# Prompt attention: diagonal blocks first in each unit, and the order 3, 2, 0, 1 for the last head and the output

## The chip, the cores and the metric

The kernel runs on one core of a Trainium2 chip. The metric is device time in microseconds (us) of one execution; lower is better. All tensors are float32. The engines are named as the profile names them: PE (TensorE, matmuls), DVE (VectorE), ACT (ScalarE), POOL (GpSimd) and SP (SyncE, which here only issues DMAs). Each engine works through its own instructions strictly in the order in which the program lists them; engines wait for one another through semaphores.

## The reference, cut to what matters

One layer of a hybrid decoder: a prompt of 2048 tokens and 64 sample tokens go through an input projection, a latent attention with 8 heads (MLA), a gated linear attention (GLA), an output projection, a gated addition and a norm. The change touches the attention of the prompt, and the order in which the output stage takes the prompt's tiles.

```python
def block(args):
    qn_b, qr_b, start = args
    s = (jnp.einsum('bqhd,bkhd->bhqk', qn_b, k_nope)
         + jnp.einsum('bqhr,bkr->bhqk', qr_b, k_rope)).astype(jnp.float32) * scale
    qpos = start + jnp.arange(Q_BLOCK)
    s = jnp.where(kpos[None, :] <= qpos[:, None], s, -jnp.inf)
    p = jax.nn.softmax(s, axis=-1).astype(v.dtype)
    return jnp.einsum('bhqk,bkhd->bqhd', p, v)
...
h = h + jnp.concatenate([o_mla, o_gla], axis=-1) @ w_out
h = h + jax.nn.sigmoid(h @ w_ple_gate) * (p_l @ w_ple_proj)
```

## The kernel before, in words

The kernel runs in stages: projections and GLA (to about 790 us of the span), then the attention of the prompt with the attention of the sample tokens (`decode`) woven into its first heads, then the output stage (`output`), tile by tile.

**Units.** The attention of the prompt is cut into 32 units (h, j): head h from 0 to 7, and for each head the query tile j of 512 queries, in the order `JS = (3, 2, 1, 0)`. A unit (h, j) reads the keys up to its own last query: 4j + 4 blocks of 128 keys. The 4j earlier blocks are full (512 queries wide). The last four lie on the diagonal: they are 512, 384, 256 and 128 queries wide, and a triangle of 128 x 128 in each has to be set to zero. So a unit with j = 0 has nothing but diagonal blocks.

**One block** (`attend`, L944): three matmuls make the scores in a PSUM tile `psC` of which there are two (L955 to L957); two exponentials on ACT write `ph`, rounded for the matmul, and `pf`, in full precision (L959, L961); a subtraction on DVE makes the low part `pl` from both (L963); in a diagonal block two selects on POOL zero the triangle, first of `ph`, then of `pl` (L966); then three matmuls, called PV here, add to the output tile `poC` (L968 to L970). There is **one** `poC` (`bufs=1`): the next unit's first PV waits until ACT has copied it out as `ob` (L973). A tile of `psC` is free again when `pf` has been made from it. The reading of `ph` by the subtraction comes before the select of `ph`, so a select waits for L963.

**The maxima** of the next unit (`maxima`, L915) run between the blocks of the current one: matmuls into `pmC` (L925), reductions on DVE (L927, L930, L932), and at the end a negation (L937), four small matmuls that turn the result (L940) and a copy by ACT into row 96 of the next unit's queries (L941), without which its first scores cannot start.

**After a unit** `ob` goes to DRAM: the values to `Od`, the sums to `Dd` (L974, L975). After the last unit of a head, and after every unit of head 7, the sums are read back (L980), inverted on DVE (L981) and written to `Rd` (L982).

**The output stage** splits its weights into a high part (on POOL, `gcopy`, L52) and a low part (DVE, L61). The first of them, from `in_w_out`, go into the places of keys and values that are already free, while head 7 still runs: they are loaded into `VT0`, head 6's values, once (6, 0) has finished. For each tile of 128 tokens `mix` (L1068) loads `Od`, `Gd`, `Rd` and `MGd` into four tiles `raw` (L1072 to L1079), multiplies on POOL (L1082) and DVE (L1083), and transposes on PE into `ptE` (L1087); `outproj` and `ple` are matmuls into `pgE`. The first three tiles' `mix` is begun while head 7 runs.

**The order of the work** on each engine is made when the program is built: a scheduler with a model of the time places the instructions, so the order around a place can change although the code there does not.

## Time and profile before

| | |
|---|---|
| median of 3 runs | 1880.7 us (1877.29 to 1881.57) |
| the profiled execution | 1881.52 us; its span, from the first instruction to the last, 1879.5 us |
| mean granted clock of PE in it | 0.955 |
| chain that ended last, PE's share | 70% |

The page counts a matmul as busy for the whole time from its start to its modelled end. Matmuls overlap, so the time at which the next one starts is what counts, and a wait of PE is longer than the idle time that the page shows for it. The page's PE row shows some digits below 9 within the span: at the start, around 750 to 800 us, and between 1375 and 1425 us, where attention ends and the output begins.

The view of stretches gives busy time of each engine and the granted clock in any part of the span. The timeline lists instructions one by one with the idle time before them and what ended it. Both are used below.

### The profile page before, as it was taken

What the parts mean: (1) busy time and instruction counts of PE and PEld (TensorE: products, weight loads), DVE (VectorE), ACT (ScalarE), POOL (GpSimd) and SP (SyncE); (2) the same over time, 40 slices, a digit from 0 to 9 for tenths busy, and PEclk for the clock granted to TensorE, in tenths of its full rate; (3) what the DMA queues carried; (4) which work ended last, traced back from release to release, by engine and by line L of the source; (5) the groups of instructions that cost most, each with busy time, mean ns of one, the idle gap of its engine ahead of it and who ended that gap; (6) DMA issues with size and microseconds to landing.
All of it is one profiled execution on the core that took longest, in us unless ns stands there. A gap on an engine that the chain in (4) does not pass through costs nothing.

```text
span 1879.5 us, 26843 instructions
## 1 busy us (share of the span) xinstructions
PE 1749.4 (93%) x8928; PEld 1365.5 (73%) x8928; DVE 1080.3 (57%) x2359; ACT 781.7 (42%) x1896; POOL 532.3 (28%) x915
## 2 busy tenths in 40 slices
PE   4999987899999998499999999999999999999996
PEld 3877776688887786266666777777777888888884
DVE  6376476466653666466666687777777333333323
ACT  4354365343431433055554666766661212121212
POOL 5253253333442334424343011111136000000000
PEclk7999989899999998699999999999998999999998
DMA  5164475511111114655666243123334223322111
GB/s 170 40 241 140 163 272 183 170 42 40 45 40 48 32 35 121 195 157 155 184 172 171 62 129 89 49 69 77 91 84 147 89 75 88 95 85 82 56 49 34
DMA packets 187748, 200.53 MB, mean 107 GB/s; under 512 B 23290, under 2 KB 130668, under 8 KB 187612
## 3 DMA queue, kind: packets, MB, share of 16 engines
q1 hardware_dynamic: 180956, 177.86, 32.3%
q0 software_dynamic: 6656, 20.98, 3.6%
q8 instruction: 71, 1.16, 0.3%
q14 instruction: 65, 0.53, 0.1%
HBM read 142.42 MB, written 56.35 MB: 106 GB/s over the span
## 4 chain that ended last, share of the span: by engine, by line
PE 70%; DMA 3%; DVE 3%; issue 2%; SPq 1%; POOL 1%; ACT 1%; POOLq 0%; ACTq 0%; DVEq 0%
PE pgE L64 7%; PE pgE L66 7%; PE pgE L65 7%; PE pgB L66 4%; PE pgB L64 4%; PE pgB L65 4%; PE psC L955 3%; PE poC L968 3%; PE pmC L925 3%; PE poC L970 3%; PE psC L957 3%; PE psC L956 3%; PE poC L969 3%; PE ptD L783 2%; PE poD L82 1%
## 5 line engine op out<-in xcount | busy, mean ns | idle before, releaser
L959 ACT ACTIVATE ph<-psC 128x512 fp32r<-128x512 f32 (+1 forms) x320 | 171.5, 536 | 206.1 <-PE psC L957 90.1
L963 DVE TENSOR_TENSOR pl<-pf,ph 128x512 fp32r<-128x512 f32 (+1 forms) x320 | 191.3, 608 | 58.5 <-ACT pf L961 49.2
L961 ACT ACTIVATE pf<-psC 128x512 f32<-128x512 f32 (+1 forms) x320 | 170.9, 534 | 0.0
L927 DVE TENSOR_REDUCE mxC<-pmC 128x1 f32<-128x512 f32 x192 | 128.9, 684 | 54.0 <-PE pmC L925 38.1
L955 PE MATMUL psC<-qC,KT 97*128 97x512 f32 (+1 forms) x320 | 124.1, 388 | 15.4 <-issue 11.8
L966 POOL TENSOR_SCALAR_AFFINE_SELECT ph<-ph 128x128 fp32r<-128x128 f32 x128 | 43.3, 339 | 322.5 <-DVE pl L963 228.0
L968 PE MATMUL poC<-ph,VT 128*128 128x512 f32 (+1 forms) x320 | 124.3, 388 | 8.8 <-POOL ph L966 6.7
L925 PE MATMUL pmC<-KT,qC 96*128 96x512 f32 (+2 forms) x320 | 119.2, 399 | 10.1 <-issue 4.6
L970 PE MATMUL poC<-pl,VT 128*128 128x512 f32 (+1 forms) x320 | 122.0, 382 | 1.3 <-DVE pl L963 1.3
L956 PE MATMUL psC<-qC,KT 96*128 96x512 f32 (+1 forms) x320 | 119.6, 374 | 0.0
L957 PE MATMUL psC<-qC,KT 96*128 96x512 f32 (+1 forms) x320 | 119.5, 373 | 0.0
L969 PE MATMUL poC<-ph,VT 128*64 128x512 f32 (+1 forms) x320 | 118.1, 369 | 0.0
L955 PEld LDWEIGHTS psC<-qC,KT 97*128 97x128 f32 x320 | 61.3, 192 | 38.4 <-issue 13.4
L1139 DVE SCALAR_TENSOR_TENSOR thE<-thE,pgE 128x512 f32<-128x512 f32 x32 | 22.0, 688 | 114.3 <-ACT thE L1138 114.3
L64 PE MATMUL pgE<-wpg,hh 128*128 128x512 f32 x224 | 87.7, 392 | 0.0
L65 PE MATMUL pgE<-wpg,hh 128*128 128x512 f32 x224 | 87.7, 392 | 0.0
L925 PEld LDWEIGHTS pmC<-KT,qC 96*128 96x128 f32 x320 | 62.6, 198 | 32.3 <-issue 11.0
L1138 ACT ACTIVATE thE<-pgE 128x512 f32<-128x512 f32 x32 | 19.1, 598 | 160.6 <-PE pgE L66 160.6
L66 PE MATMUL pgE<-wpg,hl 128*128 128x512 f32 x224 | 85.3, 392 | 0.0
L968 PEld LDWEIGHTS poC<-ph,VT 128*128 128x128 f32 x320 | 62.7, 196 | 29.0 <-POOL ph L966 13.4
L775 POOL DMA_INDIRECT kt<-in_kropeT,idk x64 | 61.5, 961 | 65.5 <-PE ptD L787 49.5
L61 DVE TENSOR_TENSOR x<-x 128x512 fp32r<-128x512 f32 (+2 forms) x74 | 64.6, 917 | 22.8 <-PE pgB L65 14.2
(456 smaller groups left out, 4674.7 us busy)
## 6 DMA issues: line engine op xcount, KB each, us to landing
x<-in_xT SPq DMA_DIRECT2D x32, 512.0 KB
ct<-in_ckvT SPq DMA_DIRECT2D x256, 64.0 KB
x<-in_w_in SPq DMA_DIRECT2D x16, 512.0 KB
Qn<-qq SPq DMA_DIRECT2D x16, 512.0 KB
Kn<-qq SPq DMA_DIRECT2D x16, 512.0 KB
Vd<-qq SPq DMA_DIRECT2D x16, 512.0 KB
KT<-Kn SPq DMA_DIRECT2D x32, 256.0 KB
VT<-Vd SPq DMA_DIRECT2D x8, 1024.0 KB
```

What stands on the lines that cost most here:

```text
L64: T_.matmul(out, ah, bh, start=first, stop=False)
L65: T_.matmul(out, ah, bl, start=False, stop=False)
L66: T_.matmul(out, al, bh, start=False, stop=last)
L925: T_.matmul(ps[:, :w], qs, kv[0][cb][:96, 0, :w], start=True, stop=True)
L955: T_.matmul(ps[:, c0:], kh[:, ks], qh[:, c0:], start=True, stop=False)
L956: T_.matmul(ps[:, c0:], kh[:96, ks], ql[:, c0:], start=False, stop=False)
L957: T_.matmul(ps[:, c0:], kl[:, ks], qh[:96, c0:], start=False, stop=True)
L959: A.activation(ph[:, c0:], ps[:, c0:], AF.Exp, scale=SC)
L963: V.tensor_tensor(pl[:, c0:], pf[:, c0:], ph[:, c0:].bitcast(F32), op=ALU.subtract)
L968: T_.matmul(o[:, c0:], vt[:, kb, DV:192], ph[:, c0:], start=kb == 0, stop=False)
L969: T_.matmul(o[:DV, c0:], vt[:, kb, 0:DV], ph[:, c0:], start=False, stop=False)
L970: T_.matmul(o[:, c0:], vt[:, kb, DV:192], pl[:, c0:], start=False, stop=kb == nk - 1)
```

## The change

In `attend` the loop over the key blocks now starts with the four diagonal blocks and then takes the full ones; the flags that open and close the accumulation follow the new first and last block. Head 7 takes its query tiles in the order 3, 2, 0, 1 (`LAST`), and the output stage takes its tiles in the same order, so that its last prompt tiles are those of j = 1. The arithmetic of each block, the number of matmuls, exponentials, selects and DMAs, and their sizes are the same.

```diff
-            for kb in range(nk):
+
+            for n, kb in enumerate(list(range(4 * j, nk)) + list(range(4 * j))):
                 dg = kb - 4 * j
...
-                T_.matmul(o[:, c0:], vt[:, kb, DV:192], ph[:, c0:], start=kb == 0, stop=False)
+                T_.matmul(o[:, c0:], vt[:, kb, DV:192], ph[:, c0:], start=n == 0, stop=False)
                 T_.matmul(o[:DV, c0:], vt[:, kb, 0:DV], ph[:, c0:], start=False, stop=False)
-                T_.matmul(o[:, c0:], vt[:, kb, DV:192], pl[:, c0:], start=False, stop=kb == nk - 1)
+                T_.matmul(o[:, c0:], vt[:, kb, DV:192], pl[:, c0:], start=False, stop=n == nk - 1)
...
-            if h == H - 1 or j == 0:
+            if h == H - 1 or j == JS[-1]:
                 n = 4 if h == H - 1 else 16
-                view = slice(j * 512, j * 512 + n * P)
+                c0 = j * 512 if h == H - 1 else 0
+                view = slice(c0, c0 + n * P)
...
-        units = [(h, j) for h in range(H) for j in JS]
+        units = [(h, j) for h in range(H) for j in (JS if h < H - 1 else LAST)]
...
-            tiles = [(j * 4 + q, P) for j in JS for q in range(4)] + [(NT, SD)]
+            tiles = [(j * 4 + q, P) for j in LAST for q in range(4)] + [(NT, SD)]
...
 JS = (3, 2, 1, 0)
+LAST = (3, 2, 0, 1)
```

The lines of `attend` after the loop's head stand one lower in the changed file, those of the output stage two lower (the scores are L956 to L958, the PV matmuls L969 to L971, the select L967, `ob` L974, `mix`'s product on POOL L1084). In the rows below a number behind a name tells one tile from another.

**Place 1, PE and ACT between two heads**, from (4, 0) to (5, 3). `poC_12191` is the output tile of (4, 0), `psC_12347` the first scores of (5, 3), `qC_12188` its queries, `m4r_12322` its maxima. PE before:

```order
L968 MATMUL poC_12191<-ph_12255,VT0_6777 128x256
L969 MATMUL poC_12191<-ph_12255,VT0_6777 64x256
L940 MATMUL pmC_12324<-identr_73,m4r_12322 1x128 x4
L925 MATMUL pmC_12375<-KT10_6773,qC_12343 128x512
L970 MATMUL poC_12191<-pl_12259,VT0_6777 128x256
L968 MATMUL poC_12191<-ph_12295,VT0_6777 128x128
L969 MATMUL poC_12191<-ph_12295,VT0_6777 64x128
L970 MATMUL poC_12191<-pl_12299,VT0_6777 128x128
L955 MATMUL psC_12347<-qC_12188,KT10_6773 128x512
```

PE after the change, and behind it ACT there, before and after:

```order
L969 MATMUL poC_12191<-ph_12295,VT0_6777 128x128
L970 MATMUL poC_12191<-ph_12295,VT0_6777 64x128
L971 MATMUL poC_12191<-pl_12299,VT0_6777 128x128
L940 MATMUL pmC_12324<-identr_73,m4r_12322 1x128 x4
L925 MATMUL pmC_12379<-KT10_6773,qC_12343 128x512
L956 MATMUL psC_12347<-qC_12188,KT13_6776 128x512
```

```order
L961 ACTIVATE pf_12257<-psC_12251 128x256
L959 ACTIVATE ph_12295<-psC_12291 128x128
L961 ACTIVATE pf_12297<-psC_12291 128x128
L941 ACTIVATE qC_12188<-pmC_12324 1x512
L973 ACTIVATE ob_12330<-poC_12191 128x512
L959 ACTIVATE ph_12351<-psC_12347 128x512
```

```order
L962 ACTIVATE pf_12257<-psC_12251 128x256
L960 ACTIVATE ph_12295<-psC_12291 128x128
L962 ACTIVATE pf_12297<-psC_12291 128x128
L974 ACTIVATE ob_12330<-poC_12191 128x512
L941 ACTIVATE qC_12188<-pmC_12324 1x512
L960 ACTIVATE ph_12351<-psC_12347 128x512
```

The small matmuls of the maxima moved behind the last PV of the unit, and on ACT the copy of the maxima moved behind `ob`.

**Place 2, POOL at the start of head 7.** `KT00` to `KT03` are the first places of the output's weights, `VT0` holds what was loaded for them; `ph_14376`, `ph_14391` and `ph_14430` belong to the first diagonal blocks of (7, 3) after the change, `ph_14614` to the first diagonal block of (7, 3) before it. Before:

```order
L52 TENSOR_SCALAR KT00_15230<-VT0_15211 128x512
L52 TENSOR_SCALAR KT01_15233<-VT0_15211 128x512
L52 TENSOR_SCALAR KT02_15237<-VT0_15211 128x512
L52 TENSOR_SCALAR KT03_15240<-VT0_15211 128x512
L966 AFFINE_SELECT ph_14614<-ph_14614 128x128
```

After the change:

```order
L52 TENSOR_SCALAR KT00_15230<-VT0_15211 128x512
L52 TENSOR_SCALAR KT01_15233<-VT0_15211 128x512
L52 TENSOR_SCALAR KT02_15237<-VT0_15211 128x512
L52 TENSOR_SCALAR KT03_15240<-VT0_15211 128x512
L967 AFFINE_SELECT ph_14376<-ph_14376 128x128
L967 AFFINE_SELECT pl_14380<-pl_14380 128x128
L52 TENSOR_SCALAR KT13_15244<-VT0_15211 128x512
L967 AFFINE_SELECT ph_14391<-ph_14391 128x128
```

The four splits stand where they stood, behind the selects of head 6; but the select that follows them belongs to the first block of (7, 3) now, and belonged to its 13th before.

**Place 3, POOL near the end of attention.** `raw_15377`, `raw_15453` and `raw_15632` are the products of the first, second and third output tile. Before, `ph_14870` and `ph_14900` are the first two diagonal blocks of (7, 2), in its second half:

```order
L1082 TENSOR_TENSOR raw_15377<-raw_15377,raw_15379 128x512
L966 AFFINE_SELECT ph_14870<-ph_14870 128x128
L966 AFFINE_SELECT pl_14874<-pl_14874 128x128
L52 TENSOR_SCALAR KT12_15251<-VT0_15211 128x512
L52 TENSOR_SCALAR qC_15254<-VT0_15211 128x512
L966 AFFINE_SELECT ph_14900<-ph_14900 128x128
L966 AFFINE_SELECT pl_14904<-pl_14904 128x128
L1082 TENSOR_TENSOR raw_15453<-raw_15453,raw_15455 128x512
```

After the change, `ph_14966` is the first block of (7, 0) and `ph_15090` the first of (7, 1), the last unit; `pl_15052` is the last diagonal block of (7, 0):

```order
L1084 TENSOR_TENSOR raw_15377<-raw_15377,raw_15379 128x512
L52 TENSOR_SCALAR qC_15254<-VT0_15211 128x512
L1084 TENSOR_TENSOR raw_15453<-raw_15453,raw_15455 128x512
L967 AFFINE_SELECT ph_14966<-ph_14966 128x128
...
L967 AFFINE_SELECT pl_15052<-pl_15052 128x128
L1084 TENSOR_TENSOR raw_15632<-raw_15632,raw_15634 128x512
L967 AFFINE_SELECT ph_15090<-ph_15090 128x128
```

The first product has no select right behind it any more; the second stands ahead of the first block of (7, 0), and the third ahead of the first block of the last unit.

## The prediction

> **What bounds the kernel now.** I read the page first, then the view of stretches, then the chain of waits for what one matmul costs, and last the timeline at the ends of units.

> ```profile
> span 1879.5 us, 26843 instructions
> PE 1749.4 (93%) x8928; PEld 1365.5 (73%) x8928; DVE 1080.3 (57%) x2359; ACT 781.7 (42%) x1896; POOL 532.3 (28%) x915
> ```

> PE is busy for 93% of the span and no other engine for more than 73%. The change adds and removes no work, so it can only alter how long PE waits. The profiled execution took 1881.5 us, 2.0 us more than its span and 0.8 us over the median of 1880.7; all sums below are against 1881.5. The stretches show where waiting remains:

> ```profile
> core 0: us, PE busy (x) PEld busy (x) DVE busy (x) ACT busy (x) POOL busy (x), PEclk, DMA share, GB/s
> 801.00:1104.80 303.80, 296.52 (x1789) 206.78 (x1788) 194.30 (x601) 167.34 (x362) 98.54 (x170) 0.97 0.55 152
> 1163.90:1224.60 60.70, 59.88 (x299) 47.58 (x297) 46.93 (x122) 41.80 (x89) 8.86 (x32) 1.00 0.28 69
> 1285.70:1346.40 60.70, 59.88 (x300) 47.59 (x297) 46.96 (x122) 41.82 (x89) 8.84 (x32) 1.00 0.23 57
> 1346.40:1375.20 28.80, 27.46 (x127) 20.51 (x125) 24.13 (x53) 18.68 (x39) 7.21 (x14) 1.00 0.32 103
> 1375.20:1421.80 46.60, 38.49 (x162) 29.32 (x162) 31.59 (x64) 25.48 (x56) 20.52 (x36) 0.82 0.36 93
> 1391.70:1398.50 6.80, 6.54 (x21) 5.29 (x22) 6.67 (x13) 2.40 (x7) 6.62 (x11) 0.50 0.41 113
> 1412.20:1421.80 9.60, 7.83 (x28) 6.10 (x28) 5.88 (x9) 3.95 (x10) 7.97 (x19) 0.50 0.17 38
> 1421.80:1425.80 4.00, 4.00 (x10) 3.13 (x11) 3.98 (x4) 0.00 (x0) 3.44 (x4) 0.50 0.48 140
> ```

> Heads 4 and 6 take 60.7 us each, at full clock, with 0.8 us of idle PE. The end of attention, from the last PV of (7, 3) to the first output matmul, takes 46.6 us with 8 us idle and the clock at 0.82. So the tail has much to win, and a steady head little; a steady head can lose.

> **What a wait of PE really is.** The chain of waits gives the step from one matmul to the next:

> ```profile
> 1157.16 0.18 PE psC L957
> 1163.24 0.24 PE pmC L940 x4
> 1163.95 0.06 PE poC L969
> 1164.65 0.23 PE psC L956
> 1157.86 0.12 PE poC L968
> ```

> A width of 512 costs 0.235 us (0.23 and 0.24 alternate), 384 costs 0.18, 256 costs 0.12, 128 from 0.06 (PV) to 0.11 (scores), the four L940 0.24. I count each stretch of PE's order with these steps and call the rest lost.

> **Steady heads, 3 to 6.** Rows at (3, 1), (3, 0) and (4, 3):

> ```profile
> 1158.69 0.22 PE L970 MATMUL poC<-pl,VT 128*128 128x128 f32 x1
> 1159.12 0.51 ACT L961 ACTIVATE pf<-psC 128x384 f32<-128x384 f32 x1
> 1159.49 0.63 ACT L973 ACTIVATE ob<-poC 128x512 f32<-128x512 f32 x1
> 1159.69 0.33 PE L955 MATMUL psC<-qC,KT 97*128 97x128 f32 x1
> 1160.92 0.50 PE L968 MATMUL poC<-ph,VT 128*128 128x512 f32 x1 [0.40 <-POOL ph L966]
> 1163.52 0.58 ACT L941 ACTIVATE qC<-pmC 1x512 fp32r<-1x512 f32 x1 [1.32 <-PE pmC L940]
> 1163.85 0.27 PE L970 MATMUL poC<-pl,VT 128*128 128x128 f32 x1
> 1164.15 0.50 PE L955 MATMUL psC<-qC,KT 97*128 97x512 f32 x1
> ```

> Three rules follow. `ob` comes when the last PV has ended and ACT is free, and the next PV 0.05 after `ob`. The 128-wide scores wait for the 384-wide `pf` (1159.12 + 0.51, then 1159.69), because there are two `psC`. The first scores of a head start 0.05 after L941. One block's chain takes its lengths from here:

> ```profile
> L963 DVE TENSOR_TENSOR pl<-pf,ph 128x512 fp32r<-128x512 f32 x126 | 85.0, 685 | 22.0 <-ACT pf L961 19.6 <-issue 2.1
> L961 ACT ACTIVATE pf<-psC 128x512 f32<-128x512 f32 x126 | 75.2, 597 | 0.0
> L927 DVE TENSOR_REDUCE mxC<-pmC 128x1 f32<-128x512 f32 x107 | 71.2, 683 | 18.4 <-PE pmC L925 18.4
> L966 POOL TENSOR_SCALAR_AFFINE_SELECT ph<-ph 128x128 fp32r<-128x128 f32 x72 | 23.5, 327 | 224.8 <-DVE pl L963 140.2 <-DVE mxC L919 55.7 <-PE pmC L925 28.8
> ```

> I follow each engine's new order at head 4 with these, by hand.
> - From j = 3 to 2: PE has only one maxima matmul and the 256- and 128-wide scores (0.9 us) between the last PV and the next; before it had 1.6 us. `ob` stands behind the 384-wide exponentials. About 0.5 us lost, where the same count finds 0.1 now: **+0.4**.
> - From 2 to 1: 0.2 against 0.1, **+0.1**.
> - From 1 to 0: the first PV, now at 2.23 us behind the last (1158.69 to 1160.92), waits for two reductions in front of its subtraction. In the new order they stand behind it, and the PV goes at about 1.2: **-1.0**.
> - In (h, 0): the other three blocks' subtractions come behind those reductions, in a queue with fewer matmuls beside it; 1.2 us lost against 0.75: **+0.4**.
> - Between heads (place 1): L940 is behind the last PV and L941 behind `ob`. Last PV, 0.3 to its end, `ob` 0.6, L941 0.58: the scores start 1.5 us behind the last PV, not 0.3 (1163.85 to 1164.15), with 0.5 of work between. Then the 256-wide scores wait 0.5 for the first `pf`, those behind 0.2. Lost 1.8 against 0.3: **+1.5**.

> Together +1.4 for a head, four times: **+5.6**. Further, the reciprocal of a head's sums now stands ahead of the fourth diagonal subtraction of the next head. Before, it came 8.3 us after the start of `ob` (1224.88 to 1233.16); PE needs that block 8 us after it:

> ```profile
> 1224.88 0.60 ACT L973 ACTIVATE ob<-poC 128x512 f32<-128x512 f32 x1
> 1233.16 0.94 DVE L981 RECIPROCAL rcC<-rcC 16x128 f32<-16x128 f32 x1 [1.86 <-DMA rcC<-Dd]
> ```

> That is 0.7 us of new wait against some 0.2 now, for three heads: **+1.5**. Bounds for the steady heads: 0, if the scheduler's fill covers what I count by hand as bare, and +13.

> **The start of head 7** (place 2).

> ```profile
> 1351.67 2.80 POOL L52 TENSOR_SCALAR KT<-VT 128x512 fp32r<-128x512 f32 x4 [5.73 <-DMA VT<-in_w_out]
> 1355.67 0.50 PE L970 MATMUL poC<-pl,VT 128*128 128x512 f32 x1 [1.09 <-DVE pl L963]
> ```

> The splits wait for a load that starts when (6, 0) has ended, and are over at 1354.5, 8.1 us after the last PV of head 6 (1346.4). No select is near now; afterwards the select of the very first block is behind them, and PE needs it 5.6 us after that PV. So 2.8 us of wait appear. Against that stands the 1.1 us (second row), with another 0.5 around it, which falls to the new wait: **+1.2**. A wait of this length can halve the clock, which the next part prices: **+2.5**. Bounds 0 and +8.

> **The tail.**

> ```profile
> 1375.64 0.63 ACT L973 ACTIVATE ob<-poC 128x512 f32<-128x512 f32 x1
> 1384.75 0.65 PE L1087 MATMUL ptE<-ident,raw 128*128 128x128 f32 x4 [0.17 <-DMA raw<-MGd]
> 1384.28 0.62 SPq L1077 DMA_DIRECT2D raw<-Rd  x1
> 1388.88 1.27 POOL L1082 TENSOR_TENSOR raw<-raw 128x512 f32<-128x512 f32 x1 [14.19 <-DMA raw<-Rd]
> 1391.96 0.80 PE L968 MATMUL poC<-ph,VT 128*128 128x512 f32 x1 [2.09 <-DVE mxC L930]
> 1409.65 0.94 DVE L981 RECIPROCAL rcC<-rcC 4x128 f32<-4x128 f32 x1 [2.95 <-DMA rcC<-Dd]
> 1412.35 0.69 PE L968 MATMUL poC<-ph,VT 128*128 128x384 f32 x1 [2.64 <-POOL ph L966]
> 1421.77 0.79 PE L64 MATMUL pgE<-KT,mh 128*128 128x512 f32 x1 [0.69 <-ACT ob L973]
> ```

> PE's order from the last PV of (7, 3) on holds 87 steps of 512, 20 of 384, 19 of 256, 19 of 128, eight L940 and eight transposes: 28.8 us, and 1.1 for the last `ob`. It takes 47, so 17 us are lost: waits of 2.1 us (a subtraction behind L1083, which waits for POOL and a load of `Rd`) and 2.6 us (behind a reciprocal), smaller ones, and half clock after both (the two stretches at 0.50 above), which goes on for 4 us of the output and costs 2 more.

> The new order has 29.3 us of steps. The two waits go, and others come. The transposes of the first output tile stand 7.7 us behind the last PV, not 9.2; their load landed 9.1 us after `ob` started (1375.64 to 1384.75): 1.7 us of wait. The product of the third tile (place 3) needs a load of `Rd` whose second half is issued behind the stores of (7, 2)'s `ob`: 1.7 us after that `ob` starts, 4.5 until it lands (the load ahead of 1388.88 was issued at 1384.28), 1.3 for the product, 0.3 for the select: 7.8. PE is there after 5.5 to 6: 2 us of wait. The chain of (7, 0) and the second transposes I put at 2, the reciprocal of (7, 0) at 1, ends of units at 1, half clock at 5 to 6. That is 13 to 14 instead of 19: **-5**. Bounds: -12 if the clock stays up and the loads land in time, +3 if all waits halve it.

> The clock: after waits of 2.09 and 2.64 us it fell to half for 6.8 and 13.6 us; after the 1.09 us at 1355.67 the stretch stays at 1.00. A halving of 5 us costs 2.5; I count it for waits over 1.5 us with 0.75.

> [...]

> **Heads 0 to 2** stand between the sample attention's instructions (303.8 us, clock 0.97, 7.3 us idle). POOL's selects there share a queue with gathers. I find no reason for either sign: 0, with 6 us either way.

> **The sum**: 5.6 + 1.5 + 3.7 - 5 + 0 = +5.8 on 1881.5: **1887 us**, 0.3% over the median.

> **Rivals.**
> - *Tail wins.* The steady losses are covered (0), head 7's start costs 1, the tail gives 12: 1881.5 - 11 = 1870. For it: 17 us of loss lie in the tail and only 0.8 us of visible idle in a head. Against: between heads L941 stands behind `ob` in an order that cannot move. It decides where L941 starts within 0.3 us of the last PV.
> - *Even.* The tail gives 8, head 7 keeps its clock: 7 + 1.2 - 8: 1882.
> - *Half clock at every head.* Between heads some 3.5 us of loss fall into 8 us; if that halves the clock for 6.8 us, four heads cost 3.4 each: 1887 + 13.6 = 1900. Now 1.9 us lost in 4.5 do not do it (clock 1.00 for heads 4 and 6), so it is not the forecast.

> [...]

> That the order does not change is excluded by the listings.

> **Chances.** Forecast 0.40, half clock 0.12, even 0.25, tail 0.23. The forecast alone spans 1885 to 1892 us; the range goes from 1874, inside the tail's case, to 1899, near the third rival. A measurement can tell 0.2% (3.8 us) from no change. Forecast and half clock lie above that, the even case within it, the tail below: faster 0.23, same 0.25, slower 0.52.

> **What would show it.** Heads 4 to 6 at 62 to 63 us in place of 60.7; first scores of a head 1.5 us behind the last PV; a wait of PE on POOL's select at the start of (7, 3); the tail near 42 us, with waits on `MGd` and on the third product. Wrong, if heads stay at 60.7 us or if the tail falls under 37.

## The result, and the profile after

The changed kernel took 1907.9 us (median of 4 runs, 1901.0 to 1913.2) against 1880.4 for the kernel before: ratio 1.0144, 95% interval 1.0122 to 1.0165. It is slower, by four to five times what was forecast, and outside the range. The first lines are from the page of the changed kernel.

```profile
span 1905.1 us, 26858 instructions
PE 1758.7 (92%) x8928; PEld 1372.0 (72%) x8928; DVE 1083.0 (57%) x2359; ACT 783.4 (41%) x1896; POOL 535.0 (28%) x915
```

The span grew by 25.6 us with the same number of matmuls. The view of stretches, cut at the start of each head's last `ob`, shows where. The rows are heads 0 to 2 (from the first scores), heads 3, 4, 5 and 6, unit (7, 3), the rest of head 7, and the output; columns as in the view before.

```profile
797.70:1111.20 313.50, 302.43 (x1800) 211.77 (x1801) 197.80 (x608) 169.45 (x366) 97.98 (x170) 0.95 0.54 150
1111.20:1171.70 60.50, 57.84 (x284) 45.49 (x284) 45.11 (x117) 39.66 (x84) 9.09 (x32) 1.00 0.26 68
1171.70:1234.50 62.80, 60.98 (x301) 47.84 (x298) 47.25 (x121) 42.35 (x89) 8.99 (x32) 1.00 0.26 69
1234.50:1300.60 66.10, 64.90 (x298) 51.29 (x296) 47.44 (x121) 42.14 (x88) 8.98 (x32) 0.92 0.25 65
1300.60:1365.70 65.10, 63.48 (x299) 50.15 (x297) 47.44 (x121) 42.20 (x88) 8.98 (x32) 0.95 0.21 53
1365.70:1400.30 34.60, 31.28 (x133) 23.56 (x131) 25.61 (x59) 19.36 (x39) 7.78 (x15) 0.85 0.30 86
1400.30:1443.20 42.90, 36.70 (x157) 27.40 (x156) 31.14 (x57) 24.89 (x55) 18.94 (x34) 0.88 0.37 96
1443.20:1905.10 461.90, 441.02 (x1996) 357.96 (x1996) 170.93 (x243) 89.63 (x189) 53.15 (x88) 0.98 0.27 81
```

The same cuts in the kernel before, beside what was predicted:

| stretch | before | after | measured | predicted |
|---|---|---|---|---|
| heads 0 to 2 | 307.9 | 313.5 | +5.6 | 0 |
| heads 3 to 6 | 58.2 + 60.7 + 61.1 + 60.7 = 240.7 | 60.5 + 62.8 + 66.1 + 65.1 = 254.5 | +13.8 | +5.6 + 1.5 |
| (7, 3) | 28.9 | 34.6 | +5.7 | +3.7 |
| rest of head 7 | 45.5 | 42.9 | -2.6 | -5 |
| output | 458.4 | 461.9 | +3.5 | 0 |

With 0.4 us less ahead of attention this is the 25.6. Heads 3 and 4, at full clock, lost 2.3 and 2.1 us, near the forecast (1.9); heads 5 and 6 lost 5.0 and 4.4 and have a clock of 0.92 and 0.95. The timeline of the changed kernel shows the single waits; what follows PE's idle time in brackets is what ended it.

```profile
935.47 0.94 DVE L983 RECIPROCAL rcC<-rcC 16x128 f32<-16x128 f32 x1 [5.30 <-DMA rcC<-Dd]
937.08 0.79 PE L925 MATMUL pmC<-KT,qC 96*128 96x512 f32 x1 [2.24 <-DVE mxC L927]
1120.44 0.94 DVE L983 RECIPROCAL rcC<-rcC 16x128 f32<-16x128 f32 x1 [2.52 <-DMA rcC<-Dd]
1121.98 0.51 PE L971 MATMUL poC<-pl,VT 128*128 128x512 f32 x1 [1.56 <-DVE pl L964]
1234.09 0.33 PE L971 MATMUL poC<-pl,VT 128*128 128x128 f32 x1
1235.71 0.50 PE L956 MATMUL psC<-qC,KT 97*128 97x512 f32 x1 [0.77 <-ACT qC L941]
1244.08 0.94 DVE L983 RECIPROCAL rcC<-rcC 16x128 f32<-16x128 f32 x1 [2.16 <-DMA rcC<-Dd]
1374.89 0.80 PE L969 MATMUL poC<-ph,VT 128*128 128x512 f32 x1 [1.95 <-POOL ph L967]
1410.61 0.69 PE L1089 MATMUL ptE<-ident,raw 128*128 128x128 f32 x2 [2.42 <-DMA raw<-MGd]
1432.70 0.50 PE L969 MATMUL poC<-ph,VT 128*128 128x512 f32 x1 [1.70 <-POOL ph L967]
```

The waits that the prediction named are there: the scores of a new head 1.6 us behind the last PV (1234.09 to 1235.71), (7, 3)'s first select, the load of `MGd`, the third product. What it did not have are the first four rows. In head 1, DVE stood 5.3 us at the reciprocal of head 0's sums, because `Dd` had not been read back; the reductions behind it came late, and PE waited 2.24 us, in the midst of 13.6 us of half clock (932.4 to 946.0) that a wait of 1.94 us, ended at 930.23, had begun. That first wait has another cause: it stands, as long, in the run with the late reciprocal below (at 932.12). Head 3 starts without a wait on L941; its loss is mostly the 1.56 us behind the reciprocal of head 2's sums, so its agreement with the forecast is luck.

### The profile page after: what moved, and what is told of

It reads as the page before. It is cut to its first block, busy times and chain, and to the rows that moved or that the text cites. A ratio compares the mean times of both kernels' runs of the same rounds, so it can differ in the third digit from the quotient of the medians.

```text
span 1905.1 us, 26858 instructions
## 1 busy us (share of the span) xinstructions
PE 1758.7 (92%) x8928; PEld 1372.0 (72%) x8928; DVE 1083.0 (57%) x2359; ACT 783.4 (41%) x1896; POOL 535.0 (28%) x915
## 4 chain that ended last, share of the span: by engine, by line
PE 69%; DMA 3%; DVE 3%; issue 2%; ACT 1%; SPq 1%; POOL 1%; POOLq 0%; ACTq 0%; DVEq 0%
PE pgE L64 7%; PE pgE L66 7%; PE pgE L65 7%; PE pgB L66 4%; PE pgB L64 4%; PE pgB L65 4%; PE poC L969 4%; PE psC L956 3%; PE poC L971 3%; PE psC L957 3%; PE psC L958 3%; PE pmC L925 3%; PE poC L970 3%; PE ptD L783 2%; PE poD L82 1%
## 5 line engine op out<-in xcount | busy, mean ns | idle before, releaser
L964 DVE TENSOR_TENSOR pl<-pf,ph 128x512 fp32r<-128x512 f32 (+1 forms) x320 | 194.3, 610 | 60.7 <-ACT pf L962 52.2
L927 DVE TENSOR_REDUCE mxC<-pmC 128x1 f32<-128x512 f32 x192 | 129.2, 684 | 59.2 <-PE pmC L925 40.8
L956 PE MATMUL psC<-qC,KT 97*128 97x512 f32 (+1 forms) x320 | 126.4, 395 | 18.6 <-issue 12.7
L967 POOL TENSOR_SCALAR_AFFINE_SELECT ph<-ph 128x128 fp32r<-128x128 f32 x128 | 42.4, 331 | 346.1 <-DVE pl L964 193.2
L925 PE MATMUL pmC<-KT,qC 96*128 96x512 f32 (+2 forms) x320 | 121.6, 411 | 12.8 <-DVE mxC L927 4.9
L969 PE MATMUL poC<-ph,VT 128*128 128x512 f32 (+1 forms) x320 | 126.2, 394 | 6.0 <-POOL ph L967 4.6
L971 PE MATMUL poC<-pl,VT 128*128 128x512 f32 (+1 forms) x320 | 123.0, 385 | 3.2 <-DVE pl L964 3.2
L957 PE MATMUL psC<-qC,KT 96*128 96x512 f32 (+1 forms) x320 | 122.7, 383 | 0.0
L958 PE MATMUL psC<-qC,KT 96*128 96x512 f32 (+1 forms) x320 | 121.9, 381 | 0.0
L970 PE MATMUL poC<-ph,VT 128*64 128x512 f32 (+1 forms) x320 | 119.0, 372 | 0.0
L956 PEld LDWEIGHTS psC<-qC,KT 97*128 97x128 f32 x320 | 63.9, 200 | 43.2 <-issue 14.4
L925 PEld LDWEIGHTS pmC<-KT,qC 96*128 96x128 f32 x320 | 64.0, 204 | 33.4 <-issue 12.4
L64 PE MATMUL pgE<-wpg,hh 128*128 128x512 f32 x224 | 87.6, 391 | 0.0
L969 PEld LDWEIGHTS poC<-ph,VT 128*128 128x128 f32 x320 | 63.1, 197 | 26.7 <-POOL ph L967 12.5
L971 PEld LDWEIGHTS poC<-pl,VT 128*128 128x128 f32 x320 | 62.5, 195 | 24.3 <-DVE pl L964 5.5
```

What stands on the lines that cost most here:

```text
L64: T_.matmul(out, ah, bh, start=first, stop=False)
L925: T_.matmul(ps[:, :w], qs, kv[0][cb][:96, 0, :w], start=True, stop=True)
L956: T_.matmul(ps[:, c0:], kh[:, ks], qh[:, c0:], start=True, stop=False)
L957: T_.matmul(ps[:, c0:], kh[:96, ks], ql[:, c0:], start=False, stop=False)
L958: T_.matmul(ps[:, c0:], kl[:, ks], qh[:96, c0:], start=False, stop=True)
L964: V.tensor_tensor(pl[:, c0:], pf[:, c0:], ph[:, c0:].bitcast(F32), op=ALU.subtract)
```

## The experiments

The runs were made in three sets, on chips on which the kernel before took 1853.5, 1880.8 and 1876.4 us; so ratios to it are compared, and expectations in us are read against the 1880 of the time before.

**First set: which part, which place.** In the first run the order 3, 2, 1, 0 is kept everywhere:

```diff
-LAST = (3, 2, 0, 1)
+LAST = (3, 2, 1, 0)
```

> Diagonal blocks first, but head 7 and the output in the old order 3, 2, 1, 0. Theory W (the copy of the maxima, late between two heads, makes PE wait about 2 us a head, and some of these waits put the clock to half for one to three stretches of 3.41 us): the loss stays, 1898 to 1910 us; heads 3 to 6 at 62.5 us, or at 65 to 66 where the clock falls. Rival T (the new order of the last head and of the output costs it): 1880 to 1888 us.

Measured: 1.0151 (1.0127 to 1.0175). The loss stays. Heads 4 to 6 took 62.9, 63.7 and 63.8 us here, all at full clock; in heads 5 and 6 PE waited 1.13 and 1.30 us behind the reciprocal. So the loss does not need half clock in these heads. The second run has the other part alone:

```diff
-            for n, kb in enumerate(list(range(4 * j, nk)) + list(range(4 * j))):
+            for n, kb in enumerate(range(nk)):
```

> Blocks in rising order as before, only head 7 and the output in the order 3, 2, 0, 1. Theory W: heads 3 to 6 at 60.7 us at full clock, 1876 to 1887 us in all. Rival T: 1893 us or more, with the loss in the end of attention or in the output.

Measured: 1.0020 (1.0010 to 1.0031), with heads 4 to 6 at 60.7 to 60.9 us. So the blocks' order costs nearly everything. Both ran on one chip, and their stretches for heads 0 to 2, the row of the first run ahead of the second's, differ by 11 us:

```profile
785.70:1091.60 305.90, 294.62 (x1800) 205.43 (x1801) 198.84 (x609) 169.60 (x366) 105.66 (x178) 0.98 0.56 157
```

```profile
785.10:1079.90 294.80, 291.30 (x1799) 203.41 (x1800) 196.50 (x606) 168.56 (x365) 106.54 (x179) 0.99 0.59 162
```

On this chip the largest part lies where I had found no reason for either sign. Next, the changed kernel with query tile 3 as before:

```diff
-            for n, kb in enumerate(list(range(4 * j, nk)) + list(range(4 * j))):
+            for n, kb in enumerate(range(nk) if j == 3 else [*range(4 * j, nk), *range(4 * j)]):
```

> The changed kernel, but the units of query tile 3 take their blocks in rising order as before, so that the first block of a head is a wide one and L941 stands ahead of ob again. Theory W: heads 3 to 6 at 60.5 to 61 us at full clock and no wait for a select at the start of head 7: 1880 to 1890 us. Rival S (the loss sits in every unit that starts with its diagonal blocks): heads at 62 us or more, 1895 to 1905 us.

Measured: 1.0093 (1.0070 to 1.0116). The heads did what theory W says, the total did not. Head 4 from the stretches, and two rows of the timeline in head 1:

```profile
1150.90:1211.40 60.50, 59.92 (x296) 47.60 (x296) 46.94 (x122) 42.07 (x89) 8.56 (x32) 1.00 0.27 71
```

```profile
898.99 0.94 DVE L983 RECIPROCAL rcC<-rcC 16x128 f32<-16x128 f32 x1 [8.22 <-DMA rcC<-Dd]
900.60 0.80 PE L971 MATMUL poC<-pl,VT 128*128 128x512 f32 x1 [5.18 <-DVE pl L964]
```

Heads 4 to 6 are back at 60.5 to 60.7 us, but heads 0 to 2 take 304.5 us: DVE stands 8.22 us at the reciprocal and PE waits 5.18 us behind it, and the same comes again in head 2 (4.93 us). Then the late copy of the maxima:

```diff
-            acc = 0.0
+            acc = steps / 4 if mg is not None and j == 0 else 0.0
```

> The changed kernel, but between the blocks of a unit with j = 0 the maxima of the next head's first unit start one block earlier, so that L940 stands two PV matmul groups ahead and L941 ahead of ob; the blocks stay diagonal first. Theory W: the first scores of a head come 0.3 us behind the last PV, heads 3 to 6 at 60.7 to 61.5 us at full clock, 1888 to 1896 us in all (head 7's start and the output stay as they are). Rival S: heads at 62 us or more, within 3 us of the changed kernel's 1908.

Measured: 1.0147 (1.0114 to 1.0179). Theory W fell as the main cause. Its wait did go, and another took its place, in head 4 of this run:

```profile
1150.86 0.50 PE L956 MATMUL psC<-qC,KT 97*128 97x512 f32 x1 [0.15 <-ACT qC L941]
1159.82 0.94 DVE L983 RECIPROCAL rcC<-rcC 16x128 f32<-16x128 f32 x1 [2.74 <-DMA rcC<-Dd]
1161.06 0.95 PE L925 MATMUL pmC<-KT,qC 96*128 96x512 f32 x2 [1.49 <-DVE mxC L932]
```

The scores wait 0.15 us in place of 0.77. But the reciprocal cannot come before `Dd` is read back, 9.0 us after `ob` (1150.83). PE, which is earlier now, waits 1.49 us there, and 2.15 in head 5. Two waits stand one behind the other, and the second ended only with the read-back of `Dd`, at 1159.82.

**Second set: the reciprocal.** The new theory, R, is that most of the loss stands behind this reciprocal. To move it, its result goes into a tile that is first written by a small copy of a later block's `pf` (16 x 128; the reciprocal overwrites it). The load of `Dd` is issued where it was.

```diff
+        def inverse(dep=None):
+            h, view, n, rc = late.pop()
+            ri = rc
+            if dep is not None:
+                ri = sp.tile([16, P], F32, name="riC")
+                V.tensor_copy(ri[:n], dep[:n, 0:P])
+            V.reciprocal(ri[:n], rc[:n])
+            nc.sync.dma_start(Rd[h, view].rearrange("(a b) -> a b", b=P), ri[:n])
...
+                if late and n == 9:
+                    inverse(pf)
...
-                V.reciprocal(rc[:n], rc[:n])
-                nc.sync.dma_start(Rd[h, view].rearrange("(a b) -> a b", b=P), rc[:n])
+                late.append((h, view, n, rc))
+                if h == H - 1:
+                    inverse()
```

> The changed kernel with only the reciprocal of a finished head's sums moved: it goes behind a small copy that needs block 10 of the next head's first unit, so it stands six blocks later in DVE's queue (its load is issued as before); heads 0 to 6. Theory R (most of the loss is DVE standing at this reciprocal until Dd has been read back, with the new order needing sooner what is queued behind it; in heads 0 to 2 waits of 2 to 6 us, with half clock after them): no such wait is left, heads 0 to 2 shorter by 5 to 9 us, heads 3 to 6 at 61.7 to 62.3 us; ratio to before 1.004 to 1.009. Rival W (the late copy of the maxima between heads): ratio 1.013 to 1.016, unchanged.

Measured: 1.0052 (1.0036 to 1.0069), from 1.0144. Rival W is out as the main cause. Heads 4, 5 and 6 by the stretches:

```profile
1165.10:1225.80 60.70, 59.78 (x295) 47.36 (x295) 47.18 (x122) 41.68 (x88) 8.86 (x32) 1.00 0.28 71
1225.80:1290.80 65.00, 63.37 (x299) 50.07 (x296) 48.00 (x122) 42.27 (x88) 8.86 (x32) 0.95 0.25 66
1290.80:1355.80 65.00, 63.38 (x299) 50.09 (x297) 47.98 (x122) 42.28 (x88) 8.86 (x32) 0.95 0.22 54
```

Head 4 is at the 60.7 us of the kernel before, better than expected. But its start is not the one of the changed kernel: the scheduler, given another program, put L941 ahead of `ob` there, and the first scores do not wait.

```profile
1164.20 0.58 ACT L941 ACTIVATE qC<-pmC 1x512 fp32r<-1x512 f32 x1 [1.17 <-PE pmC L940]
1164.87 0.46 PE L967 MATMUL psC<-qC,KT 97*128 97x512 f32 x1
1165.07 0.60 ACT L987 ACTIVATE ob<-poC 128x512 f32<-128x512 f32 x1 [0.29 <-PE poC L984]
```

Heads 5 and 6 still have L941 behind `ob` and the wait of 0.77 us, and take 65.0 us at a clock of 0.95. Each has 6.8 us at half clock, which costs 3.4 if half of it is lost (by a 512-wide step of 0.43 us at half clock, 1245.42 to 1245.85 in the changed kernel's profile, against 0.235 at full it would be 3.1); so without it they would take 61.6 us by estimate, 0.9 more than head 4. The run therefore changes two things, the place of the reciprocal and, at one head, that of L941. With the early maxima as well:

> The early maxima of the run before and the late reciprocal together. Theory R with W as the second, smaller wait: heads 3 to 6 at 60.7 to 61.3 us at full clock, as before the change; ratio 1.001 to 1.006. If neither is the cause (rival S, the narrow blocks at a unit's start themselves): heads at 62 us or more, ratio above 1.010.

Measured: 1.0022 (1.0006 to 1.0038). Heads 4 to 6 and (7, 3):

```profile
1164.80:1226.20 61.40, 60.19 (x297) 47.56 (x296) 47.52 (x123) 42.33 (x89) 8.93 (x32) 1.00 0.28 73
1226.20:1287.80 61.60, 60.39 (x297) 47.75 (x297) 47.73 (x123) 42.31 (x89) 8.93 (x32) 1.00 0.27 69
1287.80:1349.30 61.50, 60.37 (x296) 47.73 (x296) 47.64 (x123) 42.24 (x88) 8.93 (x32) 1.00 0.22 55
1349.30:1380.60 31.30, 28.86 (x127) 21.90 (x127) 24.96 (x60) 19.45 (x42) 8.08 (x15) 0.95 0.28 93
```

None of heads 3 to 6 has half clock any more. Heads 4 to 6 take 61.4 to 61.6 us, a little over what was expected, more than head 4 of the run before, and as much as its heads 5 and 6 by the estimate without half clock. So in these heads the early maxima won what the clock had cost, and no more. The control is the kernel before with the same late reciprocal:

> The kernel before with the same move of the reciprocal: what the wait costs without the change. Theory R: little, since behind it in DVE's queue stands nothing that PE needs at once: ratio 0.995 to 1.001, heads 3 to 6 at 60.6 to 60.8 us. If the wait costs the kernel before as much as the changed one, the ratio is 0.990 or lower.

Measured: 0.9985 (0.9972 to 0.9999). The same move is worth 0.15% to the kernel before, and 0.9% to the changed one. In the kernel before DVE stood there too, 3.65 us in head 1:

```profile
923.70 0.94 DVE L981 RECIPROCAL rcC<-rcC 16x128 f32<-16x128 f32 x1 [3.65 <-DMA rcC<-Dd]
```

but no wait of PE over 0.3 us followed this row. The last run of the set is the one with query tile 3 rising, with the late reciprocal:

> The run with query tile 3 in rising order, and the late reciprocal. There PE waited 5.2 and 4.9 us behind this reciprocal in heads 1 and 2, with 6.8 us of half clock after each: theory R takes these 15 to 17 us away, less what stands next: ratio 0.998 to 1.004 against 1.009. If the decode's own instructions set the time there: 1.007 or more.

Measured: 1.0047 (1.0031 to 1.0063). It missed its expectation by a little. The two long waits went, but the scheduler, given a different program, put L941 behind `ob` again: a wait of 0.77 us at the start of each of heads 4 to 7, heads 4 to 6 at 61.7 us, and one of 2.07 in (7, 3).

**Third set: the rest, and the clock.** The run with both edits, and (7, 3) alone in rising order:

```diff
-            for n, kb in enumerate(list(range(4 * j, nk)) + list(range(4 * j))):
+            for n, kb in enumerate(range(nk) if (h, j) == (7, 3) else [*range(4 * j, nk), *range(4 * j)]):
```

> The run with the early maxima and the late reciprocal (ratio 1.0022), and unit (7, 3) alone takes its blocks in rising order as before, so that its first select no longer stands right behind the splits that wait for the output's weights. Theory: the wait of 1.5 us on that select and the half clock after it go, and (7, 3) takes 28.3 to 29 us from ob to ob in place of 31.3; ratio 0.999 to 1.002. If it is not this wait: (7, 3) stays above 30.5 us.

Measured: 1.0010 (0.9998 to 1.0021), and (7, 3) at full clock:

```profile
1342.90:1370.90 28.00, 26.56 (x124) 20.49 (x124) 23.94 (x59) 18.92 (x39) 7.29 (x14) 1.00 0.32 103
```

28.0 us in place of 31.3. In the run before, PE waited 1.53 us on that select and then had 3.4 us of half clock, which costs 1.7: together 3.2 of the 3.3 us. The ratios of the two runs overlap, so the step is shown by this row, not by the totals. Then the changed kernel once more, and the one with the late reciprocal:

> The changed kernel itself once more. Theory of the gate's grid (the clock is set anew every 3.41 us from the stretch before; whether the waits between two heads fall into one stretch or two depends on where the grid lies in this execution): half-clock stretches lie on one grid of 3.41 us, at another offset than in the first profile, and it is not the same set of heads (5 and 6, not 4) that has them. If the program itself decides: heads 5, 6 and 7 again, head 4 not.

> The run with the late reciprocal once more: there head 4 took 60.7 us and heads 5 and 6 65.0 us with the same order of instructions and the same wait of 0.77 us. Theory of the grid: a head without half clock takes 60.7 to 61.0 us whichever it is, a head with it 64 to 66; which heads have it may change. If something in heads 5 and 6 costs 4 us besides the clock: these two at 62 us or more even at full clock.

Measured, one run each: 1902.3 and 1888.2 us, beside 1876.4 for the kernel before. In the second execution of the changed kernel, heads 4, 5 and 6 were

```profile
1168.90:1231.40 62.50, 60.83 (x299) 47.75 (x297) 47.27 (x121) 42.31 (x88) 8.99 (x32) 1.00 0.26 68
1231.40:1297.60 66.20, 62.46 (x300) 48.82 (x298) 47.28 (x121) 42.34 (x89) 8.99 (x32) 0.97 0.25 65
1297.60:1363.80 66.20, 64.98 (x299) 51.38 (x297) 47.63 (x121) 42.18 (x89) 9.00 (x32) 0.92 0.21 52
```

so the same heads are slow, but head 5 for another reason: the clock held between the heads and fell only at 1244.6, 13 us after `ob`, behind the reciprocal. With the reciprocal late, the second execution repeated the first (60.7, 65.0, 65.0 us). The set of heads changed in neither, against what the theory of the grid had expected and as its rival had. The edges of half clock did lie on one grid; how its place in each execution goes with the heads that fell is told in the last section, and was found only afterwards. The second expectation also rests on a false premise: head 4 does not have the order and the wait of heads 5 and 6 (rows above; the second execution is the same in this), and neither execution has heads 5 or 6 at full clock, so what else they cost stays an estimate. Between these two executions heads 0 to 2, from the first `ob` on, differ by 11.1 us (265.0 and 253.9) and each of heads 3 to 6 by 1.1 to 1.8.

Last, the kernel before with the late reciprocal, and diagonal blocks first in the last three units only, with 3, 2, 1, 0 kept:

```diff
-            for n, kb in enumerate(range(nk)):
+            for n, kb in enumerate([*range(4 * j, nk), *range(4 * j)] if h == H - 1 and j < 3 else range(nk)):
```

> The kernel before with the late reciprocal (ratio 0.9985), and diagonal blocks first only in the last three units of head 7, in the old order 2, 1, 0. Where the changed kernel gained was the end of attention, 45.5 to 42.9 us, and with the order 3, 2, 1, 0 the output lost nothing: ratio 0.995 to 0.999. If the gain of the tail needs the order 3, 2, 0, 1: 0.9985 or more.

Measured: 0.9976 (0.9965 to 0.9988). It beats both kernels, by a quarter of a per cent over the one before. Over the late reciprocal alone (0.9985, 0.9972 to 0.9999) the intervals overlap, and the end of attention took 44.2 us there, so what these blocks add is not settled. Its end of attention and its output:

```profile
1364.20:1407.80 43.60, 36.73 (x161) 26.56 (x159) 31.06 (x64) 24.44 (x54) 18.45 (x34) 0.90 0.36 95
1407.80:1866.10 458.30, 441.17 (x1997) 358.43 (x1996) 171.97 (x243) 89.89 (x189) 51.72 (x88) 0.98 0.27 82
```

## Why the prediction was wrong, step by step

The steps of the loss, from the changed kernel down:

| kernel | ratio to before |
|---|---|
| changed | 1.0144 |
| reciprocal late | 1.0052 |
| and maxima early | 1.0022 |
| and (7, 3) in rising order | 1.0010 |

- **The step that failed: the reciprocal.** The prediction put "0.7 us of new wait against some 0.2 now, for three heads: +1.5", and for heads 0 to 2 "I find no reason for either sign". Moving it was worth more than any other step: 0.9% of the time, some 17 us, by the ratios, and 11 to 14 by two pairs of profiles (1905.1 and 1894.3, on two chips; 1900.3 and 1886.3, on one), 7 to 11 of it in heads 0 to 2 from the first `ob` on. I had the mechanism, DVE standing at L981 with what PE needs behind it, and looked for it only where a read-back takes 8 us. In head 1 of the changed kernel it took 17.4 us (`ob` at 918.11, the reciprocal at 935.47). The rows that would have shown it are in the profile of before: 3.65 us of DVE's idle time at 923.70, and 3.23 at 1030.94, with no wait of PE behind them there. How the 17 us divide is only partly shown. As waits of PE behind the reciprocal one sees 2.24 us in head 1 and 1.56 in head 3 in the first profile, and 4.03, 0.83 and 2.04 us (heads 1, 3 and 5) in the second, with half clock behind some of them. The edit also changed the order in other places: L941 at head 4, and in heads 0 to 2 a wait of 2.54 us at 1007.0 is gone that no reciprocal ended, while one of 1.89 at 973.9 is new. These shares were not separated.
- **The clock.** "Now 1.9 us lost in 4.5 do not do it" kept half clock out of the forecast for the heads, and "I count it for waits over 1.5 us" made it a matter of one wait's length. Between heads a wait of 0.77 us was enough, alone (head 5) or with one of 0.42 behind it (head 6), and in head 4 both were not. The rival at 0.12 was right in heads 5 and 6, and its price, 3.4 us a head, about what they lost over head 4 (3.3 and 2.3); in heads 3 and 4 it was not.
- **Between two heads.** The wait came as worked out (1.6 us from the last PV to the scores, 1.5 forecast; 0.42 for the 256-wide scores, 0.5 forecast), and head 4, which has both waits at full clock, lost 2.1 us where 1.9 was forecast. It comes at the starts of heads 4 to 7, so the fourth of these waits stands in the row of (7, 3), and head 3 lost its 2.3 us otherwise. To call L941 the cause was half right: taken away alone it gave nothing (1.0147), since the reciprocal's wait stands next. With the reciprocal late, head 4 takes 60.7 us without L941's wait, and heads 5 and 6 some 61.6 with it and without half clock, by the estimate above: so the wait on L941 is worth about 0.9 us a head. The other part of the 1.5, the wait of the 256-wide scores, head 4 has too (0.42 us), and gains elsewhere in the head cover it. And the order that "cannot move" did move, at that head 4. The rule that the next PV comes 0.05 us after `ob` is not in the rows beside it, where it comes 0.80 us after the end of `ob` (1160.12 to 1160.92) behind a select; the row for the first output matmul has it (1421.77).
- **The start of head 7.** Right: a wait of 1.95 us on the select (2.8 forecast), and half clock, here for 10.2 us, begun by the wait between the heads. Without that one, in the run with both edits, the wait on the select still brought 3.4 us of it.
- **The tail.** The mechanisms were right (`MGd` 2.42 us against 1.7, the third product 1.70 against 2, half clock for 10.2 us, that is 5.1, against 5 to 6). The gain was 2.6 us, half of the forecast.
- **The output.** +3.5 us were not forecast. New waits of 2.21 and 1.55 us stand in its first tiles, begun at 1470.5 and 1473.9, with 3.4 us of half clock behind them. In the second execution they were 0.72 and 1.54, and the output took 459.0 us. With the new order of tiles alone there is one of 0.55, with the new order of blocks alone none. What makes them was not tried, and stays open.

The new order of the last head and of the output won nothing here: alone it gave 1.0020 (1.0010 to 1.0031), a loss.

## What to carry to other kernels

A wait that costs nothing in one order can cost time in another: at the reciprocal of head 0's sums DVE stood 3.65 us before the change, with no wait of PE over 0.3 us behind it, and 5.30 us after it, with one of 2.24. Before an order is changed, list every instruction that stands idle for a DMA in a strictly ordered queue, in the busiest stage above all, and ask of each what is queued behind it in the new order; give such an instruction a place where its data have long arrived. Waits in a row are tested by taking away the last one first.

## What the runs showed of the hardware

```profile
1232.80:1236.21 3.41, 2.43 (x15) 1.68 (x14) 1.89 (x8) 1.18 (x2) 1.02 (x4) 0.99 0.78 188
1236.21:1239.62 3.41, 3.41 (x11) 2.85 (x11) 1.20 (x4) 2.13 (x5) 0.00 (x0) 0.50 1.12 270
1239.62:1243.04 3.42, 3.42 (x11) 2.63 (x11) 2.30 (x5) 0.38 (x2) 1.82 (x6) 0.50 0.44 119
1243.04:1246.45 3.41, 3.41 (x11) 2.83 (x10) 2.37 (x7) 1.53 (x4) 0.54 (x2) 0.51 0.18 48
1246.45:1249.86 3.41, 3.41 (x20) 2.81 (x19) 2.23 (x7) 2.47 (x5) 0.00 (x0) 1.00 0.00 0
```

One stretch with PE busy for 2.43 of 3.41 us, and the next three run at half, though PE is busy in them throughout; what sets their number was not tried. A head earlier, where the grid lies 1.3 us differently against the work, the wait of 0.77 us lies in one stretch and one of 0.42 in the next, and the clock stays up:

```profile
1171.35:1174.76 3.41, 2.65 (x16) 1.93 (x14) 0.71 (x2) 1.90 (x4) 0.00 (x0) 1.00 0.91 226
1174.76:1178.18 3.42, 2.95 (x16) 2.41 (x16) 3.42 (x8) 1.82 (x6) 1.29 (x4) 1.00 1.03 261
```

Five profiles have the wait on L941 in this order of blocks (the changed kernel twice, the late reciprocal twice, the blocks alone), at 18 starts of heads in all. Where `ob` started 1.4 to 1.8 or 2.9 to 3.3 us into a stretch of the grid, the clock fell within 4 us, all 11 times; at 0.0 to 0.5 or 2.1 to 2.8 us it did not, all 7 times. These bounds were drawn from the same 18 starts, and no run has tested them. The two executions with the late reciprocal had the same offsets against their heads to within 0.2 us, which fits that heads 5 and 6 fell in both. In the changed kernel's profile `ob` started 0.4 us into a stretch at head 4, and 1.7, 3.0 and 3.3 at heads 5, 6 and 7.

What came ahead of a fall is shown as well. Ahead of attention the clock fell at 789.0 us in the changed kernel's profile and at 790.9 in that of before, each time behind a stretch of the grid in which PE ran nothing. But each of the 14 falls in their attention and early output came behind one in which PE was busy for 26 to 76%. The share alone does not decide it: behind stretches at 54 and 58%, from 1120.1 and 898.2 on, the changed kernel kept its clock. So of the theory that the clock is set anew every 3.41 us from the stretch before, the grid is shown, and of the stretch before no more than this.

One more thing was not expected: in three runs on the chip of the first set the first scores of attention came at 785.1 to 785.7 us (order alone, tile 3 rising, blocks alone), and in the other profiles at 792 to 798, behind a wait of PE of 10 to 13 us. That wait is in the kernel before as well (11.82 us), so it is no part of the difference. What holds PE there is not shown.
